# Advancing the mixers' fibers at both halves of a compression chunk

## The chip, the cores and the metric

One core of a Trainium2 chip runs the kernel. The metric is the device time of one execution in microseconds (us). The kernel before was timed three times; its median is 1667.24 us.

## The reference, cut to what matters

One decoder layer on 256 tokens of width 4096, all in float32. A modulated input is projected once (`u @ w_in`), three kinds of mixers work on the columns of the result, and their outputs are projected back.

```python
mod = c @ w_ada[l] + b_ada[l]
shift, scale, gate = jnp.split(mod, 3, axis=-1)
u = x * (1.0 + scale[:, None]) + shift[:, None]
proj = u @ w_in[l]
(rg_x, rg_g, nsa_q, kv_c, kv_s, kv_w, nsa_gl, nsa_g,
 hg_q, hg_f, hg_i, hg_g) = jnp.split(proj, splits, axis=-1)
y_rg  = _rg_lru(_causal_dwconv(rg_x, ...), ...) * jax.nn.silu(rg_g)      # RG-LRU
y_nsa = _nsa(nsa_q, kv_c, kv_s, kv_w, nsa_gl, ...) * jax.nn.silu(nsa_g)  # sparse attention
y_hg  = _hgrn2(hg_q, hg_f, hg_i, hg_g, lbs[l], hg_norm_g[l])             # HGRN2
y = jnp.concatenate([y_rg, y_nsa, y_hg], axis=-1) @ w_out[l]
x = _layer_norm(ALPHA * x + (1.0 + gate[:, None]) * y, ln_g[l], ln_b[l])
```

Inside `_nsa`, keys and values of the compressed branch come from a small network, `silu(blk @ w1) @ w2`, whose first matrix `w1` has 4096 x 256 elements for the keys and as many for the values. Inside `_hgrn2`, a gated linear recurrence runs over the tokens; the kernel works it out in seven doubling levels (block lengths 1, 2, 4, ... 64) of small matmuls.

## The kernel before, in words

**Steps.** The whole program is one list of steps, `order`, and a loop over it at the end of `trunk` writes out the instructions. A `win` step is 1024 columns (512 KB) of `w_in`; a `wout` step is as much of `w_out`; a `cmp` step is 512 KB of `w1`. Weights are float32; `split` makes a high and a low part of each (`hi` and `lo`: two copies on ACT, the low part half on DVE, half on POOL), so that a `win` step is 24 matmuls of 128x256 (L460) and a `wout` step 12 matmuls of 128x512 (L984). A `cmp` step isn't split and is 4 small matmuls (L513). The input projection goes over the contraction in ten blocks; within the last block the 16 `cmp` steps (8 for keys, 8 for values) stand among the `win` steps, two or three `win` steps to each `cmp` step: steps 358 to 411 of the list. The first `wout` step is step 415.

**Order.** Each engine runs its instructions in the order in which the loop writes them out. An instruction that waits holds up all that stands behind it on its engine. Nothing is reordered later.

**Fibers.** The mixers are generators, called fibers: four `rg_fiber` (RG-LRU, L630 is their matmul), four `hg_fiber` (HGRN2), eight `nsa_fiber`. Each writes out a few instructions and yields. Lanes start them in turn: the first `rg` fibers while the last input block runs, `hg` fibers 0, 1 and 2 when all `rg` fibers have started, `nsa` fibers after that. An `hg` fiber has L705, then for each of its seven levels four matmuls of 128x64 (L723), a product on DVE, a product on POOL (`hgk`) and a predicated copy on DVE, then L748, L757 to L759, L771, L784, and at the end a product on DVE, a cast on ACT and a subtraction on POOL that make `yh` and `yl`, the operands of L984.

**The planner's clock.** `run_bg()` gives every live fiber one chance to go on. From the last input block on it adds 1 to `tick`. A fiber that gave work to engines isn't advanced before the tick at which, by the planner's bookkeeping, that work is done: `lapse(HALF)` takes `HALF` = 1.28 us off what each engine is booked to owe, and `advance` turns what is owed into ticks of 1.28 us. Fibers of the lanes are passed over while DVE or ACT owes more than `MAY_OWE` = 2.5 us. These numbers decide the order of the instructions alone; nothing of them is a time on the chip.

**Where ticks come from.** In each step of the last input block and later the loop calls `lapse` and `run_bg` twice: once inside the step, after its first half of matmuls has been written out, and once at its end. `cmp` steps are left out of the first of these. So there are 41 x 2 + 16 = 98 ticks over steps 358 to 414.

**The forced advance.** A `wout` step needs the mixers' outputs that it multiplies. The first five `wout` steps need those of `rg` fibers 0 to 3 and of `hg` fiber 0 (`PARTS[0]`, pairs 0, 1, 2, 3, 12). If one isn't there when the loop comes to the step, it calls `run_bg` (and `lapse`) until it is, and writes out no projection matmul meanwhile:

```python
while st.kind != "win" and not (
        st.which in CMP and live[0] < NPS if st.kind == "cmp" else st.pr in YT):
    n_ = sum(map(len, heavy))
    run_bg(lane_of(st))
    lapse(HALF)
    turns += 1
```

Of the kernel before, what the change touches and what calls it, by code (L numbers as in the profile page):

```python
# [134 lines left out]
def trunk(ctx: ExitStack, tc: tile.TileContext, pack, xT, xz, w_ada, b_row, w_in, w_out, rg_w, w1, w2,  # L135
# [22 lines left out]
    def drop(n=1):  # L158
        used[0] -= n
# [198 lines left out]
    def ada_sum():  # L358
        _, b, i, raw, _ = pending.pop(0)
        _, w, m = ADA[b]  # L360
        acc = ada_state[b]
        if b in ON_PE:

            for j in range(2):
                for h in range(2):
                    o = 32 * (2 * j + h)
                    nc.tensor.matmul(acc[0][o:o + 1, h * 256:h * 256 + 256], lhsT=vec("c", i * 2 + j),
                                     rhs=raw[:, j, h * 256:h * 256 + 256], start=i == 0, stop=i == NKT // 2 - 1,
                                     skip_group_check=True)
        for j in range(m if b not in ON_PE else 0):  # L370
            c_ = vec("c", i * m + j)
            for q, ps in enumerate(acc):
                r_ = raw[:, j, q * 512:min(w, (q + 1) * 512)]
                n = r_.shape[-1]
                if i == 0 and j == 0:
                    dve.tensor_scalar(ps[:, :n], r_, c_, None, op0=OP.mult)
                else:
                    dve.scalar_tensor_tensor(ps[:, :n], r_, c_, ps[:, :n], op0=OP.mult, op1=OP.add)
        if b >= NKB and i == NKT // m - 1:
            fibers.append([gate_end(b - NKB), 1, 0, 0, tick[0] + GATE_WAIT])  # L380
# [50 lines left out]
    for kb in range(NKB):  # L431
        state = {}
        for items, width in chunks(kb):
            st = Step("win", off, width)
# [528 lines left out]
    for pi, part in enumerate(PARTS):  # L963
        for nb in range(NB):
            state = {}
            for ci, pr in enumerate(part):
                st = Step("wout", off_o, 1024)
# [73 lines left out]
    def load(st):  # L1041
        if st.kind == "cmp":
            while len(pending) + n_cmp[0] == NRA:
                ada_sum()
            n_cmp[0] += 1
            st.raw = strm.tile([P, 1024], FT, name=nm("ra"), tag="ra", bufs=NRA)
            nc.sync.dma_start(st.raw, flat(w1, st.off, 1024))
            return
        st.raw = strm.tile([P, st.w], FT, name=nm("raw"), tag="raw", bufs=NRAW)
        nc.sync.dma_start(st.raw, flat(src_of[st.kind], st.off, st.w))  # L1050

    def split(st):
        if not st.split:
            return
        st.hi = strm.tile([P, st.w], FR, name=nm("hi"), tag="hi", bufs=NSPL)
        st.lo = strm.tile([P, st.w], FR, name=nm("lo"), tag="lo", bufs=NSPL)
        m = int(st.w * (1 - POOL_SHARE[st.i >= n_win0])) // 32 * 32
        if m <= 512 and live[0] < HP_PS:
            hp = ps_x()
            act.copy(st.hi, st.raw)  # L1060
            act.copy(hp[:, :m].bitcast(FR), st.raw[:, :m])
            pool.tensor_sub(st.lo[:, m:], st.raw[:, m:], st.hi[:, m:])
            dve.tensor_sub(st.lo[:, :m], st.raw[:, :m], hp[:, :m])
            ps_free()
            return
        act.copy(st.hi, st.raw)
        pool.tensor_sub(st.lo[:, m:], st.raw[:, m:], st.hi[:, m:])
        dve.tensor_sub(st.lo[:, :m], st.raw[:, :m], st.hi[:, :m])

    n_win0 = last0  # L1070
# [31 lines left out]
    def ada_loads(now):  # L1102
        for _ in range(8):
            if not due or due[0][0] > now + EARLY[due[0][1] >= NKB]:
                break
            t_, b, c = due[0]
            if t_ > now - (TOL if b >= NKB else 0) and (
                    len(pending) + n_cmp[0] >= NRA - (at_cmp[0] < now < at_cmp[1])
                    or (c == 0 and (len(ada_state) > 1 or live[0] + 2 > NPS))):
                break  # L1110
            due.pop(0)
            if c == 0:
                ada_begin(b)
            ada_chunk(b, c, t_)

    def ease(now):

        while pending and (pending[0][0] <= now - (TOL if pending[0][1] >= NKB else AGE)
                           or (dve.owed < SLACK and pending[0][4] <= now - SOON)):
            ada_sum()  # L1120
# [61 lines left out]
    def lane_of(st):  # L1182
        if st.kind == "cmp":
            return 3
        pr = st.pr
        return 0 if pr < 4 else 2 if pr < 12 else 1

    def lapse(us):
        for e in engines:
            e.pass_time(us)  # L1190

    def run_bg(force=None):
        tick[0] += 1 if cur[0] >= n_win0 else 2
        fibers[:] = [r_ for r_ in fibers if advance(r_)]
        for n, (lane, busy) in enumerate(zip(lanes, heavy)):
            for r_ in list(busy):
                if n != force and max(dve.owed, act.owed) > MAY_OWE:
                    continue
                if not advance(r_):
                    busy.remove(r_)  # L1200
            while len(busy) < LANES[n] and lane and tick[0] >= since[n] + STAGGER[n] and not (0 < n < 3 and lanes[n - 1]):
                need, first, cost, mk, _ = lane[0]
                if (all(x in done for x in need)
                        and used[0] + cost + sum(max(0, r_[2] - r_[3]) for h_ in heavy for r_ in h_) <= NRING - SPARE):
                    lane.pop(0)
                    since[n] = tick[0]
                    busy.append([mk(), first, cost, 0, 0])
                else:
                    break
# [28 lines left out]
    for i in range(N):  # L1238
        st, cur[0] = order[i], i
        if i + SA < N:  # L1240
            split(order[i + SA])
        if i + AHEAD < N and order[i + AHEAD].split:
            load(order[i + AHEAD])
        if i + CMP_AHEAD < N and not order[i + CMP_AHEAD].split:
            load(order[i + CMP_AHEAD])
        for f in at.pop(i, []):
            f()
        turns = 0
# [6 lines that stand above are left out]
            if turns > 40:  # L1255
                if pending:
                    ada_sum()
                ada_loads(i)
            if not n_ and not any(heavy) or turns > 3000:
                raise RuntimeError(f"stuck at {i}: {used} {live} {[list(map(len, x)) for x in (lanes, heavy)]} {len(fibers)} {len(pending)} {st.kind}")  # L1260
        for mm, post in st.work:
            for h_, _ in enumerate(mm()):
                if h_ == 0:
                    if posts:
                        posts.pop(0)()
                    if i >= n_win0 and st.kind != "cmp":
                        lapse(HALF)
                        run_bg()
            if st.kind == "wout":
                post(0)  # L1270
                posts.append(functools.partial(post, 1))
            else:
                posts.append(post)
        if st.kind == "win" and (order[i + 1].kind == "wout" or
                                 (order[i + 1].kind == "win" and order[i + 1].kb != st.kb)):
            drop(2 * ((KB[st.kb] + 1) // 2))
        lapse(HALF if i >= n_win0 else HALF * st.w / 512)
        run_bg()
        ease(i)
        ada_loads(i)  # L1280
# [143 lines left out]
```

## Time and profile before

| | |
|---|---|
| times of three runs | 1664.97, 1667.24, 1673.62 us |
| the profiled execution's own time | 1672.81 us |
| its span, first to last instruction | 1671.1 us |
| TensorE (PE) busy | 1617.8 us, 97% of the span |
| DVE, ACT, POOL busy | 1269.7, 979.2, 956.2 us |
| DMA, mean of the span | 294 GB/s |
| steps 358 to 414 of the list | about 972 to 1148 us |
| the first five `wout` steps, and what stands among them | about 1148 to 1212 us |

The span is read in stretches. A view by stretch gives the busy time of each engine, the clock that was granted to TensorE (1.00 is its upper level, 2.4 GHz, and 0.50 the lower, 1.2 GHz) and what the DMA engines moved. Matmuls are pipelined, so their durations overlap: the pace is read from start to start, not from the duration of one.

### The profile page before, as it was taken

How to read it: one execution, taken by the hardware profiler on the slowest of the kernel's cores; microseconds unless marked ns; L12 is line 12 of the kernel's file. 1: busy time of each engine (PE TensorE's matmuls, PEld its weight loads, DVE VectorE, ACT ScalarE, POOL GpSimd, SP SyncE). 2: the span in 40 equal slices, each digit the busy share in tenths (PEclk: the TensorE clock that was granted, in tenths of full speed). 3: DMA queues.
4: the chain of work that ended last, by engine and by line, in shares of the span. 5: the costliest groups of instructions: out<-in, count | busy, mean ns of one | idle time of the engine just before them, and what ended most of it. 6: DMA issues, size and time to landing. Idle time of an engine off the chain costs nothing. (4 is left out here: it accounts for less than half of the span.)

```text
span 1671.1 us, 33513 instructions
## 1 busy us (share of the span) xinstructions
PE 1617.8 (97%) x11976; PEld 1485.1 (89%) x11976; DVE 1269.7 (76%) x2219; ACT 979.2 (59%) x1565; POOL 956.2 (57%) x765
## 2 busy tenths in 40 slices
PE   6999999999999999999999999989999999999997
PEld 3999999999999999999999977778988888878884
DVE  1778988799788788788788655669479678968885
ACT  2887666655655555555555567675266556655562
POOL 1579987776655455455455446476343444555555
PEclk8999999999999999999999999999599999999998
DMA  8998989899999899899899877878067666689884
GB/s 323 363 343 297 386 300 342 300 366 342 329 341 340 289 353 334 287 344 343 294 340 333 303 257 258 284 264 305 7 211 247 236 215 212 211 292 368 327 328 152
DMA packets 146487, 491.52 MB, mean 294 GB/s; under 512 B 16264, under 2 KB 17288, under 8 KB 146320
## 3 DMA queue, kind: packets, MB, share of 16 engines
q1 hardware_dynamic: 146320, 489.38, 81.6%
q8 instruction: 94, 1.54, 0.4%
q14 instruction: 73, 0.60, 0.1%
HBM read 485.12 MB, written 4.19 MB: 293 GB/s over the span
## 5 line engine op out<-in xcount | busy, mean ns | idle before, releaser
L119 POOL TENSOR_TENSOR lo<-raw,hi 128x576 fp32r<-128x576 f32 (+4 forms) x527 | 707.7, 1345 | 600.6 <-ACT hi L119 575.1
L119 ACT CAST hi<-raw 128x1024 fp32r<-128x1024 f32 (+3 forms) x527 | 528.5, 1003 | 484.2 <-POOL lo L119 213.6
L460 PE MATMUL mm<-uh,hi 128*128 128x256 f32 x2560 | 721.0, 282 | 16.0 <-DVE lo L119 7.5
L460 PE MATMUL mm<-ul,hi 128*128 128x256 f32 x2560 | 713.8, 279 | 0.1
L460 PE MATMUL mm<-uh,lo 128*128 128x256 f32 x2560 | 713.6, 279 | 0.0
L119 DVE TENSOR_TENSOR lo<-raw,ps 128x448 fp32r<-128x448 f32 (+4 forms) x501 | 303.7, 606 | 280.1 <-ACT ps L119 215.1
L460 PEld LDWEIGHTS mm<-uh,hi 128*128 128x128 f32 x2560 | 485.6, 190 | 30.8 <-issue 12.3
L460 PEld LDWEIGHTS mm<-ul,hi 128*128 128x128 f32 x2560 | 485.3, 190 | 1.0 <-issue 0.5
L460 PEld LDWEIGHTS mm<-uh,lo 128*128 128x128 f32 x2560 | 484.2, 189 | 0.1
L119 DVE SCALAR_TENSOR_TENSOR ps<-ra,pk,ps 128x512 f32<-128x512 f32 (+1 forms) x682 | 474.3, 725 | 6.3 <-DMA ra<-in_w_ada_dram 1.0
L119 ACT CAST ps<-raw 128x448 fp32r<-128x448 f32 (+4 forms) x501 | 260.0, 519 | 0.1
L119 DVE TENSOR_TENSOR acc<-mm,acc 128x512 f32<-128x512 f32 (+1 forms) x346 | 231.2, 669 | 11.5 <-PE mm L460 11.5
L984 PE MATMUL mm<-hi,yh 128*128 128x512 f32 x512 | 210.9, 412 | 0.3 <-ACT ev L119 0.3
L984 PE MATMUL mm<-hi,yl 128*128 128x512 f32 x512 | 201.4, 393 | 0.0
L984 PE MATMUL mm<-lo,yh 128*128 128x512 f32 x512 | 200.2, 391 | 0.0
L984 PEld LDWEIGHTS mm<-hi,yh 128*128 128x128 f32 x512 | 96.5, 188 | 23.1 <-issue 5.7
L984 PEld LDWEIGHTS mm<-hi,yl 128*128 128x128 f32 x512 | 96.2, 188 | 21.3
L460 PE MATMUL mm<-hi,uh 128*128 128x256 f32 (+1 forms) x384 | 110.1, 287 | 3.9 <-DVE lo L119 2.6
L984 PEld LDWEIGHTS mm<-lo,yh 128*128 128x128 f32 x512 | 96.6, 189 | 19.0 <-issue 1.2
L460 PE MATMUL mm<-hi,ul 128*128 128x256 f32 (+1 forms) x384 | 108.4, 282 | 0.0
L460 PE MATMUL mm<-lo,uh 128*128 128x256 f32 (+1 forms) x384 | 108.4, 282 | 0.0
L119 POOL TENSOR_TENSOR acc<-ev,acc 128x512 f32<-128x512 f32 x77 | 101.0, 1312 | 2.7 <-ACT ev L119 2.3
(205 smaller groups left out, 1474.3 us busy)
## 6 DMA issues: line engine op xcount, KB each, us to landing
ra<-in_w_ada_dram SPq DMA_DIRECT2D x324, 512.0 KB, 5.7
raw<-in_w_in_dram SPq DMA_DIRECT2D x291, 512.0 KB, 4.9
raw<-in_w_out_dram SPq DMA_DIRECT2D x128, 512.0 KB, 4.7
raw<-in_w_in_dram SPq DMA_DIRECT2D x90, 384.0 KB, 4.8
ra<-in_w_ada_dram SPq DMA_DIRECT2D x64, 384.0 KB, 5.3
ra<-in_w_dram SPq DMA_DIRECT2D x16, 512.0 KB, 6.5
xz<-in_xz_dram SPq DMA_DIRECT2D x16, 256.0 KB, 5.9
out_dram<-z SPq DMA_DIRECT2D x16, 256.0 KB, 2.4
```

The costliest lines, as they stand in the source:

```text
L119: return f(*a, **k)
L460: nc.tensor.matmul(dst, lhsT=l_, rhs=r_, start=s and n_ == 0, stop=e and n_ == 2)
L984: nc.tensor.matmul(state[x], lhsT=a_, rhs=b_, start=ci == 0 and j == 0 and n_ == 0, stop=ci == len(part) - 1 and j == 1 and n_ == 2)
```

## The change

The condition that leaves `cmp` steps out of the call inside the step goes.

```diff
@@ -1263,7 +1263,7 @@
                 if h_ == 0:
                     if posts:
                         posts.pop(0)()
-                    if i >= n_win0 and st.kind != "cmp":
+                    if i >= n_win0:
                         lapse(HALF)
                         run_bg()
```

`lapse(HALF)` and `run_bg()` now run twice in each of the 16 `cmp` steps: once after its four matmuls, before anything of its end, and once at its end. Steps 358 to 414 have 114 ticks instead of 98. No instruction is added or taken away on PE, DVE, POOL or SP (10810, 2049, 770 and 1022 rows before and after); ACT has 20 loads of a function table instead of 23. What changes is where the fibers' instructions stand among the others.

On PE, where the fifth `wout` step is due. Before, the loop found `hg` fiber 0 unfinished there and advanced the fibers 27 times (once more in the step ahead). The rows below follow the last matmul of the fourth `wout` step; `hgqp` and `hgk` are operands of three `hg` fibers.

```order
L984 MATMUL mm_15913<-hi_15892,yl_15921 128x512
L723 MATMUL ps_16039<-hgqp_15788,hgk_15605 128x64 x4
L723 MATMUL ps_16057<-hgqp_15926,hgk_15835 128x64 x4
L723 MATMUL ps_16062<-hgqp_15603,hgk_15002 128x64 x4
L723 MATMUL ps_16075<-hgqp_15788,hgk_15605 128x64 x4
L723 MATMUL ps_16080<-hgqp_15603,hgk_15002 128x64 x4
L723 MATMUL ps_16089<-hgqp_15926,hgk_15835 128x64 x4
L723 MATMUL ps_16098<-hgqp_15788,hgk_15605 128x64 x4
L723 MATMUL ps_16107<-hgqp_15603,hgk_15002 128x64 x4
```

The run goes on to row 9024, 42 rows in all, with no L984 in it. Now the loop advances the fibers 6 times there, and this is all that stands between the fourth and the fifth `wout` step on PE.

```order
L984 MATMUL mm_16120<-hi_16099,yl_15350 128x512
L757 MATMUL ps_16232<-hgA_15474,acc_768 128x128
L758 MATMUL ps_16232<-hgA_15475,acc_768 128x128
L759 MATMUL ps_16232<-hgA_15474,acc_768 128x128
L757 MATMUL ps_16232<-hgA_15474,acc_768 128x128
L758 MATMUL ps_16232<-hgA_15475,acc_768 128x128
L759 MATMUL ps_16232<-hgA_15474,acc_768 128x128
L784 MATMUL ps_16259<-ident,rs_16202 128x128 x4
L771 MATMUL ps_16270<-ones,hgsq_16255 128x1 x4
L984 MATMUL mm_16108<-hi_16138,yh_16252 128x512
```

Of the 21 levels of `hg` fibers 0, 1 and 2, two stood ahead of the first L984 before, and 20 do now.

On PE, at step 404, the sixth `cmp` step of the values, which is one of eight `cmp` steps (386 to 411) that now have a live `hg` fiber. Before:

```order
L460 MATMUL mm_15427<-uh_13534,lo_15321 128x256
L367 MATMUL ps_14452<-ra_15339,pk 1x256 x4
L513 MATMUL ps_14841<-ra_15345,kpe_14676 32x256 x4
L367 MATMUL ps_14452<-ra_15341,pk 1x256 x4
L460 MATMUL mm_15495<-uh_13491,hi_15380 128x256
```

And now, with a level of each of three `hg` fibers right behind the step's own four matmuls (L367 is the gate's share of `c @ w_ada`):

```order
L460 MATMUL mm_15565<-uh_13534,lo_15430 128x256
L367 MATMUL ps_14491<-ra_15453,pk 1x256 x4
L513 MATMUL ps_14897<-ra_15459,kpe_14455 32x256 x4
L723 MATMUL ps_15611<-hgqp_15035,hgk_14842 128x64 x4
L723 MATMUL ps_15620<-hgqp_15166,hgk_15052 128x64 x4
L723 MATMUL ps_15625<-hgqp_15352,hgk_15265 128x64 x4
L367 MATMUL ps_14491<-ra_15455,pk 1x256 x4
L460 MATMUL mm_15643<-uh_13491,hi_15503 128x256
```

On the SP queue, where the first two `rg` fibers start (step 361): their loads, `rgw`, stood behind two loads of `w_ada`, one of `w_in` and one of `w1`:

```order
L340 DMA ra_13964<-in_w_ada_dram 128x1024
L340 DMA ra_13966<-in_w_ada_dram 128x1024
L1050 DMA raw_13968<-in_w_in_dram 128x1024
L1047 DMA ra_13970<-in_w_dram 128x1024
L613 DMA rgw_13985<-in_rg_w_dram 128x512
L613 DMA rgw_13992<-in_rg_w_dram 128x512
```

Now they stand ahead of these (of the two loads of `w_ada` one follows, the other comes later):

```order
L613 DMA rgw_13960<-in_rg_w_dram 128x512
L613 DMA rgw_13967<-in_rg_w_dram 128x512
L340 DMA ra_13974<-in_w_ada_dram 128x1024
L1050 DMA raw_13976<-in_w_in_dram 128x1024
L1047 DMA ra_13978<-in_w_dram 128x1024
```

## Rows read from the trace of the kernel before

**Rows 1.** The page: engine busy times, and TensorE's granted clock in 40 slices.

```profile
PE 1617.8 (97%) x11976; PEld 1485.1 (89%) x11976; DVE 1269.7 (76%) x2219; ACT 979.2 (59%) x1565; POOL 956.2 (57%) x765
...
PEclk8999999999999999999999999999599999999998
```

**Rows 2.** Busy us by stretch: stretch, length, engines, PE clock, DMA share, GB/s.

```profile
972.00:1148.00 176.00, 160.54 (x1385) 137.60 (x1384) 114.72 (x172) 123.27 (x188) 104.17 (x79) 0.96 0.78 280
1148.00:1162.00 14.00, 14.00 (x79) 12.11 (x78) 13.89 (x26) 5.16 (x7) 10.05 (x10) 1.00 0.85 298
1162.00:1209.00 47.00, 43.45 (x220) 42.94 (x219) 22.53 (x53) 8.82 (x16) 19.53 (x21) 0.56 0.12 39
1209.00:1600.00 391.00, 390.42 (x1897) 320.61 (x1897) 316.61 (x575) 231.92 (x430) 193.52 (x148) 1.00 0.74 259
```

**Rows 3.** PE in time, 1162 to 1209: start, us, instruction, records, idle and releaser.

```profile
1162.35 2.79 PE L723 MATMUL ps<-hgqp,hgk 128*128 128x64 f32 x24
1165.92 1.10 PE L723 MATMUL ps<-hgqp,hgk 128*128 128x64 f32 x8 [0.78 <-POOL hgk L119]
1168.80 10.48 PE L723 MATMUL ps<-hgqp,hgk 128*128 128x64 f32 x48 [1.78 <-DVE hgA L119]
...
1180.03 3.51 PE L723 MATMUL ps<-hgqp,hgk 128*128 128x64 f32 x16
1183.34 0.74 PE L757 MATMUL ps<-hgA,acc 128*128 128x128 f32 x2
...
1186.00 3.52 PE L723 MATMUL ps<-hgqp,hgk 128*128 128x64 f32 x16
...
1208.90 0.47 PE L984 MATMUL mm<-hi,yh 128*128 128x512 f32 x1
```

**Rows 4.** PE in time: sixteen L723 records and wide matmuls behind them, 1153 us.

```profile
1153.25 1.89 PE L723 MATMUL ps<-hgqp,hgk 128*128 128x64 f32 x16
1154.95 0.48 PE L984 MATMUL mm<-hi,yh 128*128 128x512 f32 x1
1155.26 0.39 PE L984 MATMUL mm<-lo,yh 128*128 128x512 f32 x1
1155.49 0.40 PE L984 MATMUL mm<-hi,yl 128*128 128x512 f32 x1
```

**Rows 5.** Busy us in 10 us of the third stretch, columns as in rows 2.

```profile
1170.00:1180.00 10.00, 10.00 (x48) 10.00 (x48) 7.05 (x16) 0.00 (x0) 4.85 (x6) 0.50 0.00 0
```

**Rows 6.** PE in time: around the fifteenth `cmp` step's L513.

```profile
1120.37 0.64 PE L513 MATMUL ps<-ra,kpe 128*32 128x256 f32 x8
1123.02 0.52 PE L460 MATMUL mm<-uh,hi 128*128 128x256 f32 x1 [2.02 <-DVE lo L119]
1123.34 0.42 PE L460 MATMUL mm<-ul,hi 128*128 128x256 f32 x1
...
1126.54 0.29 PE L460 MATMUL mm<-ul,hi 128*128 128x256 f32 x1
1126.67 0.28 PE L460 MATMUL mm<-uh,lo 128*128 128x256 f32 x1
```

**Rows 7.** Waits of PE, 972 to 1148: us in total, times, longest.

```profile
PE mm L460 <- DVE gate L119: 2.3, 1, 2.3
...
PE ps L630 <- DMA rgw<-in_rg_w_dram: 1.9, 1, 1.9
```

**Rows 8.** The levels' product on POOL: ns min/median/max, first and last start.

```profile
L119 POOL TENSOR_TENSOR hgk<-hgk,hgA x9: 643/802/977, 1148.8 to 1193.9; 128x256 f32<-128x256 f32 x9
```

**Rows 9.** DVE and POOL in time: the end of `hg` fiber 0.

```profile
1202.08 0.69 DVE L119 TENSOR_TENSOR hgy<-ps,hgy 128x512 f32<-128x512 f32 x1 [3.15 <-PE ps L784]
...
1203.50 1.27 POOL L119 TENSOR_TENSOR yl<-hgy,yh 128x512 fp32r<-128x512 f32 x1 [3.29 <-ACT yh L119]
```

## The prediction

> **What bounds the kernel now.** The page is read first. TensorE (PE) is busy for 97% of the span and no other engine for more than 76% [rows 1]: what can be won is PE's idle time and the time in which its clock is low. The slices of the granted clock are full but for the first, the last and one more, which is at half [rows 1]; where it lies, the view by stretch says [rows 2]: between 1162 and 1209 us the mean clock is 0.56, PE is idle for 3.6 us, and DMA moves 39 GB/s against 280 in the stretch with the `cmp` steps. After 1209 us PE has 0.6 us of idle in 391 us, at full clock.
>
> What runs in that stretch is read from PE in time [rows 3]. There is no projection matmul in it. PE has only the small matmuls of three `hg` fibers, which the loop wrote out because `hg` fiber 0 was not finished when the fifth `wout` step was due. PE counts as busy, yet at half pace: sixteen L723 records take 3.31 us from 1180.03 to 1183.34 [rows 3], and 1.70 us from 1153.25 to 1154.95 [rows 4]. The granted clock is 0.50 (1.2 GHz) in the ten microseconds from 1170, with PE busy in all of them [rows 5]. It fell after a wait of 1.78 us at 1168.80 [rows 3], and while nothing but narrow matmuls followed it stayed low.
>
> The other loss is in the stretch in which the `cmp` steps stand, 972 to 1148 us: 176 - 160.5 = 15.5 us idle, and a clock of 0.96, which is another 7 us [rows 2]. Here PE waits some 2 us at a time for DVE or for a load, 2.3 us at most [rows 7], and after such a wait it can run slow for a while: behind the wait at 1123.02 sixteen matmuls of 128x256 take 3.52 us, 0.22 each, where the next takes 0.13 [rows 6], so 1.4 us more are gone.
>
> **The change part by part.** It adds 16 ticks of the planner's clock to the 98 that steps 358 to 414 had. Every instruction stays; the fibers' stand earlier among the weights' steps. Following the loop's own bookkeeping (a count of turns, in which there is no time), the last `rg` fiber ends at step 401 instead of 418, `hg` fiber 0 starts at step 383 instead of 389 and `hg` fiber 2 at 395 instead of 413. The loop still comes to the fifth `wout` step too early for `hg` fiber 0, but has to advance the fibers 6 times and not 28.
>
> *The forced stretch, a gain.* Its loss today is the idle time, 47 - 43.45 = 3.6 us, and the low clock, (1 - 0.56) x 47 = 20.7 us, together **24.2 us** [rows 2]. The 22.8 us that are left are work at full clock that has to be done in either kernel. All sixteen levels among it stand elsewhere now; 18 levels, with two from just ahead of it, move into the stretch of the `cmp` steps. That they cost no more than themselves there is what rows 4 show: sixteen records between wide matmuls in 1.70 us, with no wait and at full clock, and from 1148 to 1162 us, where single levels of three fibers stand among `wout` matmuls, PE has no idle at all [rows 2].
>
> *What is left of it, a loss.* Between the fourth and the fifth `wout` step stand now six rows of L757 to L759 and one each of L784 and L771. The six rows take 2.66 us at half clock (1183.34 to 1186.00) [rows 3], so 1.3 at full; with the other two it is some 3 us of work. The fifth step's operands come from an L784 one step earlier: product on DVE from 1202.08, subtraction on POOL until 1204.77 in the kernel before [rows 9], 2.7 us. The work that hides it is the fourth step's twelve matmuls, 12 x 0.23 = 2.8 us by the starts in rows 4, and those 3 us. So between nothing and 5 us (the chain queued behind other work on all three engines, and a slow clock behind the wait, 1.4 us); I take **1.5**, nearer to nothing since the cover is twice the chain.
>
> *The `cmp` steps, a loss.* This is the price. A `cmp` step is 0.64 us of PE [rows 6], and the planner now books 2.56 us for it. A fiber that is let go after two ticks therefore finds its DVE and POOL work unfinished more often, and PE waits at L723 with everything behind it held up. From the eight `cmp` steps with a live `hg` fiber I take 0.5 us each, **4 us**. The nearest rows give the ends: nothing, as in rows 4; or at each of the eight the longest wait of that stretch, 2.3 us [rows 7], with 1.4 us of slow clock behind it [rows 6]: 30 us. I take a low value because the planner is slow against the chip as a whole: 98 ticks x 1.28 = 125 us are booked for 176 us [rows 2], 114 make 146 us for some 195 us (the stretch grows by some 19 us of work that moves into it: 18 levels x 0.85 us by rows 4, and about 4 us of L748 to L771). Below nothing too: the `rgw` loads move ahead of other loads on SP's queue, and a wait of 1.9 us hangs on them [rows 7]; with the 2.3 us for the gate and a slow clock behind each, -7 us.
>
> *The engines' load.* DVE is busy for 115, POOL for 104 and ACT for 123 of the 176 us [rows 2]. Into that stretch move some 28 us of DVE's work and 20 of POOL's (about three quarters of the third and second stretch together, 22.5 + 13.9 and 19.5 + 10.0 us [rows 2], part of which is the weights' own): 143 and 124 of 195 us, 73% and 64%. None becomes the bound. The loads of the weights are as many per step; at 280 GB/s before and 259 after the forced stretch [rows 2] they have room, and the 47 us in which DMA nearly rests now carry loads.
>
> One rule of the Trainium skill speaks against the change. The product of a level on POOL takes from 643 to 977 ns for the same shape [rows 8]. GPSIMD Engine Reference, section 1, Specifications, says that GpSimd shares its SBUF interfaces with VectorE and that the two contend when a VectorE instruction reads two SBUF inputs, as the levels' products on DVE do. By it each moved level's POOL product goes from its short to its long end beside the busier DVE, 18 x 0.33 = 6 us, and if PE waited for all of that the sum would be 6 us worse, 1655 instead of 1649; the spread in the row agrees with it, and cannot show it.
>
> *The sum.* -24.2 + 1.5 + 4 = -18.7 us. The profiled execution took 1672.8 us, so its like would take 1654.1. It lies 5.6 us above the median of the runs shown, which are 9 us apart; what makes these 5.6 us isn't in the trace, and I take the gain to be the same for all: 1667.2 - 18.7 = **1649 us**.
>
> **The rivals.** *The gain is larger.* The `cmp` stretch loses its two longest waits instead of getting new ones, -7 us in place of +4: 1638 us. For it speaks the earlier `rgw` load; against it that most of the 15.5 us there are waits for DVE, which gets more to do.
>
> *Half of it is given back.* The eight `cmp` steps cost 1.5 to 3 us each, 12 to 24 us in all: 1657 to 1669 us. For it speaks that three levels now follow directly on one `cmp` step's matmuls (the order in front shows it), and that PE waited 1.78 us for `hgA` where six levels stood in a row [rows 3]. Against it speaks rows 4, where two levels in a row waited for nothing.
>
> *Slower.* The same place, but with the full price: each of the 18 moved levels makes PE wait, and the clock, once fallen, is met by the next wait before it has risen. A wait of 1.78 us and 1.4 us of slow clock [rows 3, 6] at each is 57 us; that is 1667 - 24 + 1.5 + 57 = 1701 us. It decides from (24.2 - 1.5) / 18 = 1.26 us per level on. Against it: of the sixteen levels that stood together from 1162 us, with nothing between them to hide their products, only two waited on PE for longer than 0.5 us in the rows shown [rows 3].
>
> That the change doesn't do what it says is no rival: the order shows the levels moved and the forced advances gone.
>
> **How the numbers follow.** Forecast, 1642 to 1657 us: 0.60. Larger gain, 1634 to 1642: 0.14. Half given back, 1657 to 1669: 0.18, more than half of which lies under 1664. Slower, above 1675: 0.08. About 0.5%, 8 us, is what a measurement of this kernel can tell from no change, so faster is below 1659 and slower above 1675.5. Faster: 0.60 + 0.14 and a little of the third case, 0.75; slower 0.08; the rest, 0.17, is the same. The range leaves out a third of the second case at its lower end (0.05), and the last case and 0.07 of the third at its upper end (0.15): 1638 to 1664 us.
>
> **What would show it.** In the profile after, the stretch between the fourth and the fifth `wout` step should be 3 to 8 us and not 47, and the slice with the low clock gone. If it is gone and the time is still near 1667, the `cmp` stretch has got longer by more than the 19 us of moved work: look there for PE waiting on POOL `hgk` or DVE `hgA` at L723, and for a clock under 0.96. If the waits for `rgw` and for the gate are gone from that stretch, the larger gain is right. The forecast is wrong in its first step if PE's clock is low in a place of about the same length elsewhere.

## The result, and the profile after

The changed kernel takes 1652.35 us in the median (1648.70 to 1655.24), the kernel before 1669.84 us in the same measurement (1664.97 to 1673.62): a ratio of 0.9896, 95% interval 0.986 to 0.9932. That is 17.5 us less; 18.7 us were forecast. Measured once more, with more runs of the kernel before, it was 1650.85 against 1666.31 us, 0.991 (0.9881 to 0.9939), 15.5 us less.

The profiled execution took 1648.70 us (span 1647.0) at a mean clock of 0.989; that of before took 1672.81 us at 0.978. The two single executions differ by 24.1 us, more than the medians, so a second profile of each kernel was taken, and the terms below are given for both pairs.

From the page of after, the lines that answer to [rows 1]: the busy time of the engines and TensorE's granted clock in 40 slices.

```profile
PE 1600.1 (97%) x11976; PEld 1466.0 (89%) x11976; DVE 1276.6 (78%) x2219; ACT 977.2 (59%) x1564; POOL 958.7 (58%) x765
...
PEclk8999999999999999999999999999999999999999
```

The slice at half clock is gone, and PE has as many matmuls in 17.7 us less of busy time.

Busy time by stretch of after, with the columns of [rows 2]: the `cmp` steps, the first four `wout` steps, what stands between the fourth and the fifth, and the rest.

```profile
973.00:1163.70 190.70, 180.72 (x1573) 156.81 (x1565) 152.54 (x232) 120.57 (x186) 124.43 (x101) 0.97 0.73 264
1163.70:1178.00 14.30, 14.30 (x80) 12.26 (x79) 9.25 (x17) 7.90 (x12) 6.38 (x6) 1.00 0.74 227
1178.00:1182.00 4.00, 3.52 (x30) 3.33 (x29) 3.08 (x6) 3.66 (x6) 2.57 (x3) 1.00 0.89 269
1182.00:1600.00 418.00, 413.63 (x1994) 338.12 (x1994) 328.11 (x602) 248.62 (x453) 209.05 (x159) 1.00 0.76 262
```

The second profile of after, `cmp` stretch and then the first four `wout` steps with what follows them up to the fifth:

```profile
972.70:1163.40 190.70, 177.91 (x1569) 154.12 (x1561) 152.25 (x232) 120.56 (x186) 124.25 (x100) 0.99 0.72 264
1163.40:1181.40 18.00, 17.52 (x106) 15.29 (x106) 12.07 (x21) 11.43 (x18) 8.75 (x8) 1.00 0.75 237
```

The stretch of 47 us at clock 0.56 is one of 4 us at full clock, and in the second profile too the clock is full up to the fifth `wout` step. The `cmp` stretch is some 15 us longer, since the work that left the third stretch stands in it now; its PE idle time went down in spite of that, from 15.5 to 10.0 us (12.8 in the second profile). A new loss stands in the last row of the first profile: 4.4 us of idle, where [rows 2] have 0.6 us.

PE in time between the fourth and the fifth `wout` step of after: start, us, instruction, records, idle and releaser. It answers to [rows 3].

```profile
1177.72 0.39 PE L984 MATMUL mm<-hi,yl 128*128 128x512 f32 x1
1177.95 0.38 PE L757 MATMUL ps<-hgA,acc 128*128 128x128 f32 x2
...
1179.29 1.06 PE L784 MATMUL ps<-ident,rs 128*128 128x128 f32 x8
1180.83 1.05 PE L771 MATMUL ps<-ones,hgsq 128*128 128x1 f32 x8 [0.48 <-ACT hgsq L119]
1181.74 0.47 PE L984 MATMUL mm<-hi,yh 128*128 128x512 f32 x1
```

From 1177.95 to 1181.74 it is 3.8 us, with one wait of 0.48 us. No L723 stands there any more.

The longest groups of waits of PE in the `cmp` stretch of after, 973 to 1163.7 (us in total, times, longest), and then those after it, 1180 to 1600. The first answer to [rows 7].

```profile
PE mm L460 <- DVE lo L119: 5.0, 3, 3.2
PE mm L460 <- POOL lo L119: 1.2, 1, 1.2
PE ps L723 <- POOL hgk L119: 1.2, 2, 0.8
PE ps L630 <- DMA rgw<-in_rg_w_dram: 1.0, 1, 1.0
PE mm L460 <- DVE acc L119: 0.8, 1, 0.8
...
```

```profile
PE ps L902 <- DVE e L119: 1.7, 1, 1.7
PE ps L902 <- DVE lo L119: 1.0, 1, 1.0
PE ps L808 <- DVE lo L119: 0.9, 1, 0.9
...
```

The wait for the gate is gone, that for `rgw` is down from 1.9 to 1.0 us, and the moved levels at L723 wait for 1.2 us in all, 0.8 at most. The largest group of the kernel before, which [rows 7] leave out, has shrunk most, from 4.7 to 0.8 us:

```profile
PE mm L460 <- DVE acc L119: 4.7, 3, 1.9
```

### The profile page after: what moved, and what is told of

Its sections match the earlier page's. It is cut to its first block, busy times and chain, and to the rows that moved or that the text cites. A ratio compares the mean times of both kernels' runs of the same rounds, so it can differ in the third digit from the quotient of the medians.

```text
span 1647.0 us, 33506 instructions
## 1 busy us (share of the span) xinstructions
PE 1600.1 (97%) x11976; PEld 1466.0 (89%) x11976; DVE 1276.6 (78%) x2219; ACT 977.2 (59%) x1564; POOL 958.7 (58%) x765
## 4 chain that ended last, share of the span: by engine, by line
PE 82%; DVE 6%; issue 3%; DMA 3%; POOL 2%; ACT 2%; SPq 0%; DVEq 0%; POOLq 0%; ACTq 0%
PE mm L460 54%; PE mm L984 19%; DMA ra<-in_w_ada_dram 1%; PE ps L723 1%; DVE lo L119 1%; ACT hi L119 1%; DVE ps L119 1%; POOL lo L119 1%; PE ps L916 1%; PE ps L398 1%; DVE e L119 1%; PE ps L1307 1%; DMA raw<-in_w_in_dram 1%; DVE acc L119 1%; PE ps L807 1%
## 5 line engine op out<-in xcount | busy, mean ns | idle before, releaser
L984 PE MATMUL mm<-hi,yh 128*128 128x512 f32 x512 | 210.0, 410 | 0.4 <-DVE lc L119 0.4
L984 PE MATMUL mm<-hi,yl 128*128 128x512 f32 x512 | 201.2, 393 | 0.0
L984 PE MATMUL mm<-lo,yh 128*128 128x512 f32 x512 | 200.1, 391 | 0.0
L984 PEld LDWEIGHTS mm<-hi,yh 128*128 128x128 f32 x512 | 96.4, 188 | 22.6 <-issue 4.9
L984 PEld LDWEIGHTS mm<-hi,yl 128*128 128x128 f32 x512 | 96.1, 188 | 21.5
L984 PEld LDWEIGHTS mm<-lo,yh 128*128 128x128 f32 x512 | 96.5, 188 | 18.7 <-issue 0.7
```

Of the source, the lines that this page charges most:

```text
L984: nc.tensor.matmul(state[x], lhsT=a_, rhs=b_, start=ci == 0 and j == 0 and n_ == 0, stop=ci == len(part) - 1 and j == 1 and n_ == 2)
```

## The experiments

Below, the *loss* of a stretch is PE's idle time in it plus (1 - clock) x its length. Two things make it rough: the clock has two decimals, which is up to 1 us in a stretch of 200 us, and idle time under the low clock counts in both terms, so that up to half of it is counted twice. The *forced stretch* runs from the first `wout` matmul (L984) to the start of the fifth `wout` step, the *`cmp` stretch* from the first L513 to that first L984. Forced turns are the advances that the loop makes in its waiting loop because a step's input is not ready. Each row's losses are those of one profiled execution; the ratio is from several runs. The medians come from four measurements, in which before had 1669.84 (after), 1666.31 (after's second, keys, values, three), 1670.03 (warm, zero, lapse, tick) and 1665.65 us (three_room, aroom, aroom_stag2), so kernels of different measurements are compared by the ratio.

| kernel | median us | ratio to before (95%) | forced turns | loss, `cmp` stretch | loss, forced stretch |
|---|---|---|---|---|---|
| before | 1669.84 | 1 | 28 | 15.5 + 7.0 | 3.6 + 20.2 |
| before, second profile | - | 1 | 28 | 15.4 + 3.4 | 3.6 + 16.9 |
| after | 1652.35 | 0.9896 (0.986 to 0.9932) | 6 | 10.0 + 5.7 | 0.5 + 0 |
| after, second profile | 1650.85 | 0.991 (0.9881 to 0.9939) | 6 | 12.8 + 1.9 | 0.5 + 0 |
| warm | 1661.99 | 0.9946 (0.9922 to 0.997) | 28 | 14.3 + 3.4 | 0.9 + 0 |
| keys | 1651.67 | 0.9907 (0.9871 to 0.9943) | 20 | 11.8 + 1.8 | 2.7 + 1.7 |
| values | 1669.70 | 1.0018 (0.9996 to 1.0041) | 17 | 20.6 + 7.5 | 2.6 + 6.2 |
| zero | 1674.75 | 1.0017 (0.9998 to 1.0037) | 49 | 12.7 + 6.5 | 15.0 + 15.2 |
| three | 1666.27 | 1.0007 (0.9987 to 1.0027) | 0 | 21.4 + 12.9 | 0 + 0.7 |
| three_room | 1660.13 | 0.9959 (0.993 to 0.9988) | 1 | 18.1 + 10.3 | 1.0 + 0 |
| lapse | 1667.93 | 0.9996 (0.9967 to 1.0025) | 14 | 21.4 + 7.7 | 1.6 + 3.5 |
| tick | 1660.61 | 0.9926 (0.9894 to 0.9957) | 24 | 16.3 + 5.3 | 1.7 + 5.0 |
| aroom | 1654.55 | 0.9936 (0.9912 to 0.996) | 3 | 14.8 + 5.9 | 0 + 0 |
| aroom_stag2 | 1663.11 | 0.9981 (0.9953 to 1.001) | 5 | 17.7 + 14.2 | 0 + 0 |

Two theories went in. **F**: the gain is the forced stretch, at 24.2 / 28 = 0.86 us for each forced turn that is saved. **S**: more ticks spread the fibers' work better wherever they fall, at about 1 us for each added tick, whatever remains of the forced stretch.

**before and after once more.** The same two programs again, for their medians and a second profile.

> The changed kernel once more, with more rounds and a second trace. Both theories expect 17 us less than before (the gain of the first measurement, 1669.8 to 1652.4 us, where the first pair of profiled executions differed by 24). Theory F (the gain is the forced stretch between the fourth and fifth wout step: its waits and its low clock) expects in the second trace again a forced stretch of about 4 us at full clock, and a stretch of the cmp steps (973 to 1164 us) that loses 10 to 25 us by waits and low clock, the amount differing from run to run. Theory S (the extra ticks spread the fibers' work better over the stretch of the cmp steps, and the gain lies there) expects that stretch to lose again 6 us less than the 22.5 us of before.

> The kernel before once more, for a second trace. In the first the stretch from the first to the fifth wout step lost 23.8 us (3.6 waiting, 20.2 by the low clock) and the cmp stretch 22.5 us. Theory F expects the forced stretch to lose about as much again, 15 to 24 us. If it loses under 10 us here, the first trace showed a rare fall of the clock, and the 16 us between the medians need another place.

The unchanged order of before lost 20.5 us in the forced stretch this time and 23.8 the first time, and 18.8 and 22.5 us in the `cmp` stretch: the waits are the same, the clock differs. Differences between two kernels of less than some 4 us in a stretch are therefore not read as an effect. Windows of the second profile of before, columns as in [rows 2]:

```profile
1165.00:1170.00 5.00, 2.49 (x15) 2.38 (x15) 4.69 (x12) 0.00 (x0) 3.11 (x4) 0.76 0.45 148
1170.00:1200.00 30.00, 29.01 (x136) 28.82 (x136) 14.53 (x34) 4.64 (x8) 12.40 (x14) 0.50 0.03 9
1200.00:1205.70 5.70, 5.70 (x45) 5.66 (x44) 1.53 (x3) 2.33 (x5) 1.60 (x3) 0.85 0.00 0
```

The first row has half of its length idle, the second is 97% busy at 0.50: the same fall at the same wait, and 30 us of it. By the clock of 0.76 some 2.4 us of the first row are at half, so the clock fell at about 1167.6, within the wait of 1.78 us that ends at 1168.6 in this profile.

**warm: the low clock alone.** Before, with two unused matmuls of 128x512 at each forced turn; nothing moves.

```diff
             run_bg(lane_of(st))
+            if st.kind == "wout" and live[0] < NPS:
+                q, y = ps_x(), YT[0][0]
+                for _ in range(2):
+                    nc.tensor.matmul(q, lhsT=y[:, 0, :P], rhs=y.rearrange("p j t -> p (j t)"), start=True, stop=True)
+                ps_free()
```

> The kernel before, with two wide matmuls of 128x512 added to each of the 28 forced turns; their result is not used. It adds 56 x 0.23 = 13 us of work to PE and takes nothing away. If the low clock is what the forced stretch loses (theory F, 20.7 of its 24.2 us) and wide matmuls keep the clock up, the stretch gets 13 - 20.7 = 8 us shorter: 1662. If the stretch is bound by the chain through DVE and POOL (DVE is busy for 22.5 us in it) and the clock only fills the time that would be waited anyway (theory C), the clock is full but PE waits in its place, and the time is within 3 us of before or up to 13 us longer. If the added work doesn't raise the clock, 13 to 26 us longer: 1683 to 1696.

1661.99 us, 0.9946 (0.9922 to 0.997): with 56 matmuls more, some 56 x 0.23 = 12.9 us of work, the kernel is 9 us faster. The forced stretch of warm by window, and a part of it in time:

```profile
1143.90:1197.00 53.10, 52.17 (x355) 47.16 (x354) 36.16 (x78) 14.78 (x25) 29.45 (x32) 1.00 0.32 116
```

```profile
1161.29 1.00 PE L723 MATMUL ps<-hgqp,hgk 128*128 128x64 f32 x8
1162.10 1.17 PE L1256 MATMUL ps<-yh 128*128 128x512 f32 x4
...
1165.53 1.97 PE L723 MATMUL ps<-hgqp,hgk 128*128 128x64 f32 x16 [0.92 <-DVE hgA L119]
```

The clock is 1.00 throughout and sixteen L723 records take 1.97 us, where [rows 3] have 3.51. The same 28 forced turns stand in the same order. From the first to the fifth `wout` step it is 53.1 us, against 61.2 and 58.2 in the two profiles of before; less the added work it is 53.1 - 12.9 = 40.2 us, so 21 and 18 us are gone, and the low clock had been put at 20.2 and 16.9. The term of 20.7 us agrees with that. By itself warm shows that the fibers' chain needs no more than 53.1 us, so that at least 5 to 8 us were the clock's: without the added matmuls some of their 12.9 us might be waits for the chain (DVE is busy for 36 of the 53 us). keys, below, speaks against that. It has 20 such turns at nearly full clock with nothing added, and PE waits 2.7 us among them; but nine levels stand there, against nineteen in before.

**keys and values: half of the change each.** The second tick in the `cmp` steps of one of the two kinds only; each adds 8 ticks in place of 16. Both against before:

```diff
-                    if i >= n_win0 and st.kind != "cmp":
+                    if i >= n_win0 and not (st.kind == "cmp" and st.which):      # keys
...
+                    if i >= n_win0 and not (st.kind == "cmp" and not st.which):  # values
```

> The second call only in the eight cmp steps of the keys (358 to 382): 106 ticks. 20 turns are forced at the fifth wout step. Theory F: by 24 us for 28 forced turns, 20 turns lose 17 us, and the gain over before is 7 us: 1663. Theory S: half the ticks, half the gain, 9 us: 1661. What tells them apart is the trace: F expects a forced stretch of some 33 us with a low clock after the fourth wout step, S none of that size that matters and a cmp stretch with fewer waits.

> The second call only in the eight cmp steps of the values (386 to 411): 106 ticks. 17 turns are forced at the fifth wout step. Theory F: 17 turns lose 15 us, a gain of 9 us over before: 1660, and a forced stretch of some 28 us with a low clock in the trace. Theory S: half the gain, 9 us, without regard to forced turns. If neither half alone gives much and both together 17 us, the loss isn't in proportion to the turns but is one fall of the clock.

Both theories missed both. keys is as fast as the whole change, 1651.67 us, with 20 of the 28 forced turns left; values, with 17 left, gains nothing, 1669.70 us. F as a price for each turn is refuted by that, and so is S as a price for each tick. The windows of keys, `cmp` stretch, forced stretch and a part of it:

```profile
972.90:1148.70 175.80, 164.01 (x1465) 142.04 (x1458) 136.70 (x206) 117.89 (x182) 114.14 (x89) 0.99 0.78 280
1148.70:1182.50 33.80, 31.12 (x210) 28.67 (x209) 19.97 (x44) 14.58 (x23) 17.77 (x19) 0.95 0.49 173
...
1171.00:1175.00 4.00, 4.00 (x26) 4.00 (x25) 1.28 (x3) 0.38 (x2) 1.19 (x2) 0.64 0.00 0
```

PE of keys in time, where the clock falls and where it is back:

```profile
1167.69 0.68 PE L748 MATMUL ps<-hgqp,hgk 128*128 128x128 f32 x4 [0.69 <-DVE hgqp L119]
1168.21 1.00 PE L723 MATMUL ps<-hgqp,hgk 128*128 128x64 f32 x8
1170.21 1.10 PE L723 MATMUL ps<-hgqp,hgk 128*128 128x64 f32 x8 [1.00 <-DVE hgA L119]
...
1172.02 0.70 PE L757 MATMUL ps<-hgA,acc 128*128 128x128 f32 x2
...
1174.64 1.43 PE L723 MATMUL ps<-hgqp,hgk 128*128 128x64 f32 x8
...
1179.32 0.47 PE L757 MATMUL ps<-hgA,acc 128*128 128x128 f32 x2
```

Behind waits of 0.69 and 1.00 us two L757 records take 0.70 us, and 0.47 us seven us later. What costs in before is not the number of forced turns but one fall of the clock that lasts; in keys a fall is over by 1179, and the stretch loses 4.4 us, not 24.

The windows of values, and its longest groups of waits from 970 to 1200:

```profile
972.70:1161.00 188.30, 167.67 (x1449) 144.63 (x1442) 132.81 (x200) 120.94 (x182) 113.20 (x87) 0.96 0.73 261
1161.00:1197.20 36.20, 33.56 (x197) 30.72 (x197) 25.95 (x50) 12.95 (x20) 19.32 (x20) 0.83 0.45 161
```

```profile
PE ps L630 <- DMA rgw<-in_rg_w_dram: 4.5, 2, 3.3
PE ps L723 <- DVE hgA L119: 4.0, 2, 2.5
PE ps L723 <- POOL hgk L119: 3.5, 4, 1.8
```

Its forced stretch loses 9 us against 24 in the first profile of before; but its `cmp` stretch loses 28 us where before lost 19 to 23, and its rest has 4.2 us of idle. A second loss must be counted: fiber work that the order puts among the `cmp` steps before what it reads is there (of the waits above, all but 0.5 us for `hgk` are in that stretch).

**zero and three: fewer ticks and more.** zero takes the tick at the end of the `cmp` steps away too; three has three ticks in each.

```diff
# zero, against before
-        lapse(HALF if i >= n_win0 else HALF * st.w / 512)
-        run_bg()
+        if st.kind != "cmp":
+            lapse(HALF if i >= n_win0 else HALF * st.w / 512)
+            run_bg()
...
# three, against after
-                        lapse(HALF)
-                        run_bg()
+                        for _ in range(1 + (st.kind == "cmp")):
+                            lapse(HALF)
+                            run_bg()
```

> No call at all in the cmp steps (neither inside nor at their end): 82 ticks over steps 358 to 414. The loop forces 8 turns at step 386 (the first cmp step of the values, whose operand is not prepared) and 12, 11 and 18 at the third, fourth and fifth wout steps: 49 in all. Theory F expects it slower than before by the 21 more turns at 0.86 us each, 18 us: 1688, with several stretches of low clock. Theory S (the ticks of the cmp steps are what counts, evenly) expects 17 us more than before: 1687. The place in the trace tells them apart: F among the first five wout steps and at step 386, S in waits of PE for DVE or POOL in the cmp stretch.

> Three calls in each cmp step instead of two: 130 ticks over steps 358 to 414. The loop then comes to the fifth wout step with hg fiber 0 finished and forces no turn (6 with the change, 28 before). Theory F expects no further gain: the 6 forced turns of the changed kernel cost only 0.5 us of waiting, so the same time as the changed kernel within 4 us, about 1652. Theory S expects as much again as the first 16 ticks brought, about 17 us, so 1635.

zero has 49 forced turns and is slower than before by no more than the measurement can tell: 1.0017 (0.9998 to 1.0037), not by the 18 us that a price per turn gives. Its `cmp` stretch loses 19 us, as that of before, and its forced stretch 30. three has no forced turn and a forced stretch that loses 0.7 us, and yet is not faster than before: 1.0007 (0.9987 to 1.0027). What it loses stands in its `cmp` stretch, 34 us. The windows of three, and its longest groups of waits from 980 to 1198:

```profile
981.20:1196.30 215.10, 193.72 (x1645) 169.26 (x1638) 149.21 (x240) 131.10 (x206) 128.27 (x105) 0.94 0.67 236
1196.30:1212.80 16.50, 16.50 (x89) 14.21 (x89) 12.33 (x21) 9.21 (x13) 8.27 (x7) 0.96 0.60 197
```

```profile
PE ps L538 <- ACT part L119: 5.9, 2, 3.4
PE mm L460 <- DVE lo L119: 4.1, 3, 1.8
PE ps L417 <- ACT aacc L119: 3.6, 1, 3.6
PE ps L578 <- DMA w2s<-in_w_dram: 3.3, 1, 3.3
```

L538, L417 and L578 are not in the waits of after but for 0.5 us. They are matmuls of fibers whose start or pause is counted in ticks; with three ticks a step these pauses are shorter in real time, and PE comes to the matmul before `part`, `aacc` or the load is there. Nothing else of PE runs in these waits, and the clock of the stretch falls to 0.94.

**three_room: the same pauses given back.** Three, with those pauses longer in ticks.

```diff
-            fibers.append([cmp_hidden(which), 1, 0, 0, tick[0] + 1])
+            fibers.append([cmp_hidden(which), 1, 0, 0, tick[0] + 4])
...
-        yield 1
+        yield 1, PE_GAP
...
-GATE_WAIT = 4
+GATE_WAIT = 6
```

> Three calls in each cmp step, and more ticks of room for three dependent pieces: the small network's second half starts 4 ticks after its last cmp step instead of 1, its end waits a tick longer for its load, and a gate's end starts 6 ticks after its sum instead of 4. One turn is forced. Theory R (three calls lost 34 us in the cmp stretch because the planner's ticks ran ahead of ACT and the queue, so that matmuls stood in PE's order before their operands: L538, L417 and L578 waited 12.8 us for ACT and a load, with slow clock behind each) expects those waits gone and with them 12.8 us and some 8 of slow clock: 1646. Theory G (with more ticks the fibers' work simply crowds DVE, ACT and POOL, and the wait moves to whatever PE needs next) expects waits of PE for lo or acc in their place and no gain: 1666.

1660.13 us, 0.9959 (0.993 to 0.9988), against 1.0007 for three: some 6 to 8 us are won, and not 20. Theory R's price was missed, and so was G's "no gain". Its longest groups of waits, 970 to 1180:

```profile
PE ps L630 <- DMA rgw<-in_rg_w_dram: 7.3, 1, 7.3
PE mm L460 <- DVE lo L119: 4.0, 3, 1.8
PE ps L723 <- POOL hgk L119: 3.2, 1, 3.2
```

The three named groups, 12.8 us in three, are down to about 1 us. In their place PE waits 7.3 us for a load and 3.2 us for one product on POOL. So the early matmuls were a cause of what three lost, and other waits came out when they were taken away.

**lapse and tick: the planner's clock and the fibers' advance apart.** lapse lets the second tick only move the clock on, tick lets it only advance fibers.

```diff
# lapse, against after
                         lapse(HALF)
-                        run_bg()
+                        if st.kind != "cmp":
+                            run_bg()
...
# tick, against after
-                        lapse(HALF)
+                        if st.kind != "cmp":
+                            lapse(HALF)
                         run_bg()
```

> The change with lapse alone in the cmp steps: what the engines are booked to owe is let off twice, but the fibers are advanced once, as before. 14 turns are forced at the fifth wout step. Theory F, by turns: 14 turns lose 12 us, a gain of 12 over before, 1658; if the loss is one fall of the clock rather than so much per turn, the gain is smaller. Theory S (more ticks are what helps): no gain, 1670, since no tick is added.

> The change with run_bg alone in the cmp steps: the fibers are advanced twice, but what the engines owe is let off once, as before. 24 turns are forced at the fifth wout step. Theory F, by turns: 24 turns lose 21 us, a gain of 3 us, so not to be told from before: 1667. Theory S: the ticks are all there, so most of the gain, 1655.

The clock alone saves 14 forced turns and gives no gain, 0.9996 (0.9967 to 1.0025); the advance alone saves 4 and gives half of the change's gain, 0.9926 (0.9894 to 0.9957; one of its five runs took 5609.6 us, and no trace shows why). Again the number of turns doesn't order the times. lapse came out as S had it, and tick between the two theories. lapse loses 5 us in the forced stretch and 29 in the `cmp` stretch, where the longest groups of waits are these:

```profile
PE mm L460 <- DVE lo L119: 8.8, 5, 4.6
PE ps L723 <- POOL hgk L119: 5.3, 3, 2.8
```

**aroom and aroom_stag2: can the change be bettered?** The pauses of three_room (`tick[0] + 3` in place of 4) on the change, and then a start of the fibers in other ticks as well.

```diff
-STAGGER = (0, 0, 8, 0)
+STAGGER = (2, 0, 8, 0)
```

> The changed kernel with more room for the same three pieces (3 ticks instead of 1 for the small network's second half, a tick longer for its end's load, 6 instead of 4 for a gate's end); 3 turns are forced. In the changed kernel these pieces waited 0.5 us in all, so theory R expects the same time as the changed kernel within 4 us, 1651; a gain over 5 us would say that the order elsewhere is what counts.

> The same, and the rg fibers of a pair start 2 ticks apart instead of in one tick; 5 turns are forced. In the changed kernel the longest wait of PE in the cmp stretch is 3.25 us for DVE's lo, which stands behind the elementwise work of two rg fibers at once. If that work in one piece is what PE waits for, this wait and the slow clock behind it go, 3 to 8 us: 1645. If the waits are only set by how much work DVE and ACT have in the stretch, the same as the changed kernel, 1651.

Neither is faster than the change. aroom loses 20.7 us in the `cmp` stretch where after lost 15, and its forced stretch is down to nothing: the same time within 4 us. aroom_stag2 was to take 1645 or 1651 us and missed both. It loses its gain, 0.9981 (0.9953 to 1.001), in the `cmp` stretch, with a clock of 0.93 and these waits:

```profile
PE mm L460 <- DVE lo L119: 5.1, 2, 3.4
PE ps L723 <- DVE hgqp L119: 4.2, 1, 4.2
PE ps L630 <- DVE rgy L119: 3.5, 2, 2.5
```

The wait for `lo` that the later start was to take away is still there, 3.4 us at its longest.

**What the runs settle, and what stays open.** Settled: most of what before loses in the forced stretch is the low clock (warm, and keys beside it), the change takes it away, and a changed order can give the gain back in the `cmp` stretch and behind the fifth `wout` step (values, lapse, three). In profiles, the two losses together are 39 to 46 us in before, 15 to 18 in after and keys, 21 in aroom, 28 to 32 in tick, three_room and aroom_stag2, 34 to 37 in values, lapse and three, and 49 in zero. The times follow that only in the main. Warm apart, the kernels that gain are those that lose 29 us or less. But values, lapse and three should be some 2 to 12 us faster than before by this and are not, and zero, with more loss than before, can't be told from it.

A third place explains some 4 us of that for values, lapse and three: PE's idle time in the rest of the `wout` steps. It is 0.6 to 1.0 us in both profiles of before and in warm, keys, zero and tick, which have 20 forced turns or more, and 4.0 to 4.6 us in both profiles of after and in values, lapse, three, aroom and aroom_stag2, which have 17 or fewer (three_room, with one, has 1.6). It comes back so evenly that it goes with the order and is no scatter.

Open: why the `cmp` stretch loses 14 us in keys and 28 in values, which add as many ticks; their waits are at different lines, but no run moved one of them alone. Open too is why the clock stayed down for over 30 us in before and for about 4 in keys, both with narrow matmuls on a busy PE: in before it was 128x64 (L723) that came first under the low clock, in keys 128x128 (L757), but 128x128 stood in the 30 us of before as well ([rows 3] from 1183.34), and no run tried one kind against the other.

## Why the prediction was right, step by step

The forecast of 1649 us stands 3 us under the measured median, and the main case of the four came true. By its steps, with the first pair of profiles and then the second:

| step | forecast | first pair | second pair |
|---|---|---|---|
| forced stretch, loss of before | -24.2 | -23.8 | -20.5 |
| what is left of it | +1.5 | +0.5 | +0.5 |
| `cmp` steps, losses | +4 | -6.8 | -4.1 |
| moved work costs more where it stands now | 0 | +2.2 | +2.2 |
| rest of the `wout` steps | 0 | +4.3 | +4.6 |
| sum | -18.7 | -23.6 | -17.3 |

The sums go from the first L513 to the last L984; the spans of the two pairs differ by 24.1 and 19.8 us, the medians by 17.5 and 15.5.

The main step was right, and that the sum came so near is in part luck: the `cmp` steps came out 11 and 8 us better than forecast, two terms that the sum had at nothing came out 6.5 and 6.8 us worse, and the forced stretch was priced from one execution, whose clock stayed low longer than in the other.

*The forced stretch* was right in its mechanism and in its size: loop bookkeeping gave 6 forced turns, six there were, the stretch is 3.8 us and was to be 3 to 8. warm and keys show that the clock was the right thing to price. How long the clock stays down differs between executions of the same program, 20.2 and 16.9 us' worth. The Trainium skill, TensorE: Matmul & The Clock Gate, Part 1, says of this gate that "the default state is throttled, and activity releases the throttle". The clock of 1.00 in warm agrees with it. The window at 0.50 above, with PE busy for 97% of it, does not: in 30 us of what the profile counts as busy no release came. The formula for the loss counts the idle time under the low clock twice, half of some 2 us here, so that the -24.2 is about 1 us too large.

*What is left* was sized too high: the chain on DVE and POOL to the fifth step's operand was hidden, as the argument about its cover said, and what PE waited for was ACT's `hgsq`, 0.48 us.

*The `cmp` steps* were the step with the wrong sign, within its bounds of -7 to +30 us. The moved levels wait for 1.2 us in all in either profile of after, 0.15 for each of the eight steps, where 0.5 was taken. Three other waits fell in both pairs: for `acc`, from 4.7 to 0.8 us and from 4.3 to 0.8, for the gate, from 2.3 to nothing, and for a load of `w_ada` at L367, from 2.0 and 1.9 to nothing. The wait for `rgw`, which the forecast counted, fell from 1.9 to 1.0 in the first pair; in the second, 0.8 us for `rgw` gave way to 2.7 us for `rgy` at the same L630. So the rival "larger gain" was right in this stretch in its size, and in one of the two waits that it named; why `acc` and the load are there in time now, no run shows. It did not come out in the time, since two things that the sum had at nothing took 6.5 us in the first pair: the same work is 19.9 us where it was taken out at full clock and 22.1 us where it was put in, which no row explains, and the `wout` steps behind the fifth wait for DVE, 4.4 us against 0.6, at L902 and L808, matmuls of `nsa` fibers. Later work than the moved one was not looked at. A reason may be that PE, with less work ahead of them, comes to L902 and L808 earlier than DVE's results are there; that is argued, and no run tested it.

*The load on the engines* was a little low for DVE, 143 us forecast and 152.5 measured of 190.7 (80%, not 73%), and right for POOL, 124 and 124.4. No engine became the bound, as said.

*POOL's products beside a busier DVE*, the rule of the Trainium skill in GPSIMD Engine Reference, section 1, Specifications, that was to cost 6 us if it held here: of the levels' products in after the profile has, in ns as minimum, median and maximum,

```profile
L119 POOL TENSOR_TENSOR hgk<-hgk,acc x16: 617/808/1230, 1093.9 to 1263.9; 128x256 f32<-128x256 f32 x16
L119 POOL TENSOR_TENSOR hgk<-hgk,hgA x12: 621/816/1092, 1101.6 to 1254.1; 128x256 f32<-128x256 f32 x12
```

The second row is the form of [rows 8]: the median is 816 against 802 ns, the longest 1092 against 977, beside a DVE that is busy for 80% of the time in place of some 60% (36.4 of the 61 us of the second and third stretch in [rows 2]). Single products are longer, as the rule would have it; the typical one is not, and PE's waits for `hgk` are 1.2 us. The rule's price did not come.

*Half given back* and *slower* did not happen in this kernel, but the runs met the first in others. Of the five other kernels that differ only in where the ticks fall, values, lapse and three give all of the gain back and tick half of it, mainly in the `cmp` stretch, as this rival has it; keys alone keeps it. The kind of wait that it names, L723 waiting for `hgk` and `hgA`, is only a part of that: 7.0 of the 20.6 us of idle there in values, 5.3 of 21.4 in lapse, and 0.7 of 21.4 in three.

## What to carry to other kernels

A stretch in which a serial chain runs alone should be priced by the granted clock before it is priced by its waits: here 20 of 24 us were counted as clock, and filling the stretch with unused wide matmuls made the kernel faster. When work is moved out of it into a busy stretch, ask at each place whether what it reads is there by then, because an early instruction's wait holds up all that is written behind it on its engine; more of the same move (three ticks in place of two) gave the whole gain back. Profile the unchanged kernel twice before a term of a few microseconds is read as an effect, since here the same order lost 4 us more or less in one stretch.

## What was not expected of the hardware

TensorE stayed at a granted clock of 0.50 for over 30 us while it was busy for 97% of the time (1170 to 1200, in the second profile of before), with matmuls as narrow as those of [rows 3]; two 128x512 matmuls at each forced turn kept it at 1.00 in the same place (warm). In keys a fall was over after some 4 us, among matmuls of 128x128 and 128x64. Two waits of PE, of 0.69 and 1.00 us, were ahead of the fall in keys, within 5 us of it; one of 0.92 us in warm, with wide matmuls close by, brought none.
